# Attention scores Q·Kᵀ on one core: one store per head against two stores per three heads

## The chip, the cores and the metric

The kernel runs on one core of a Trainium2 chip. The metric is device time in microseconds (us) of one execution. The kernel before takes 1063.33 us, the median of three runs (1063.1 to 1064.34).

## The reference

```python
batch, n_heads, seq, head_dim = 8, 12, 1024, 64
q, k = 0.1 * randn(batch, n_heads, seq, head_dim)   # float32
out = np.einsum('bhid,bhjd->bhij', q, k)            # float32, 8 x 12 x 1024 x 1024
```

There are 96 heads. Each has Q and K of 1024 rows by 64 (256 KB each) and a result of 1024 x 1024 float32 (4 MB). Read are 50.3 MB, written 402.65 MB. Nothing is reduced on the chip: every product goes out.

## The kernel before, in words

A head's result leaves in one store. Output row 8p + t of a head lies in partition p at place t, so a store moves 128 pieces of 32 KB, one per partition, each contiguous in HBM (`scores`, line 185, issued by SyncE, called SP). The tile that it leaves from, `o_sb`, is one of three (`out_pool`, bufs=3).

To fill it, TensorE (PE) multiplies one weight tile of Q with the keys: contraction over the 64 values of `d`, 128 rows of Q, 512 keys at a time, four matmuls into a PSUM tile of 2048 columns (line 171). ScalarE (ACT) copies that to `o_sb` (line 181), four copies a head. PSUM holds two such tiles. Only the very first head uses four smaller PSUM tiles, copied by ACT and VectorE (DVE) in turn (line 179).

Q and K have to be turned, so that `d` lies along the partitions, and made float16. The 96 heads are cut into blocks of 2, 2, 4, 8, 8 and then six times 12 heads (`sizes`).

- The two blocks of 2 are loaded by head (`load_head`, line 84), cast by GpSimd (POOL, line 97) and transposed on PE, eight 128 x 128 transposes for each of Q and K (line 151), with a DVE or ACT copy out of PSUM (line 154). Both heads of a block sit side by side, 64 partitions each.
- The other blocks are loaded whole, Q and K in one DMA each (line 73). POOL casts them in quarters of 32 partitions into `half_sb` (line 127, five buffers), and DVE transposes blocks of 32 x 32 (line 145), writing them straight where PE wants them: the write goes along `i` in `dst = ... "c (i r) -> c r i"`, with R rows (32 to 96 elements of 2 bytes) from one element to the next.

What orders the work: every instruction is pinned in program order on its engine. The lists in `block` say after which matmul group of which head a transpose of the next block stands (`side`), and `LOADS` says after which head ACT issues the next two loads. SP carries the first loads of Q and all stores; ACT's queue carries the first loads of K and all later loads. A load waits for one of the two input buffers (`in_pool`), that is for POOL's casts. At the start the first 8 heads' inputs (4 MB) are loaded into the first `o_sb` buffer (`early`), and the 8 heads of block 3 (4 MB) into `x_sb`, all before the first store is issued.

Of the kernel before, what the change touches and what calls it, by code (L numbers as in the profile page):

```python
# [13 lines left out]
def kernel(  # L14
# [11 lines left out]
    GMAX = 4  # L26
    assert D == 64 and NT == 8 and BH % (2 * GMAX) == 0

# [4 lines left out]
    sizes = [2, 2, 4, 8, 8] + [12] * ((BH - 24) // 12)  # L33
    assert sum(sizes) == BH
    PE_BLOCKS = 2
    NMAX = max(sizes)
    CHUNK = 48 * 32

    consts = ctx.enter_context(tc.tile_pool(name="consts", bufs=1))
    ident = consts.tile([P, P], F16)  # L40

    in_pool = ctx.enter_context(tc.tile_pool(name="in_pool", bufs=2))
    half_pool = ctx.enter_context(tc.tile_pool(name="half_pool", bufs=5))
    tr_pool = ctx.enter_context(tc.tile_pool(name="tr_pool", bufs=2))
# [3 lines left out]

    def half_tile():
        half_sb = half_pool.tile([P, CHUNK], F16, tag="half")  # L50
        return half_sb

    class Block:

        def __init__(self, first, N, by_pe):
            self.first, self.N, self.by_pe = first, N, by_pe
            self.R = N * S // P
            self.elems = self.R * D  # L60
            self.raw = [None] * 2
            self.rows = [None] * 2
            self.halves = {}
            self.cut = max(1, self.R * 32 // CHUNK + (self.R * 32 % CHUNK > 0))

        def load(self, x, eng):
            if self.raw[x] is None:
                x_sb = in_pool.tile([P, self.elems], F32, tag="x")
                self.raw[x] = x_sb
            start = self.first * S  # L70
            src = (qf, kf)[x][start : start + self.N * S]
            pin(
                eng.dma_start(  # L73
                    out=self.raw[x], in_=src.rearrange("(p r) d -> p (r d)", p=P)
                )
            )

        def load_head(self, n, x, eng):

            start = (self.first + n) * S  # L80
            src = (qf, kf)[x][start : start + S]
            m = S * D // P
            pin(
                eng.dma_start(  # L84
                    out=self.raw[x][:, n * m : (n + 1) * m],
                    in_=src.rearrange("(p r) d -> p (r d)", p=P),
                )
            )

        def cast_rows(self, x):  # L90
            n = S * D // P
            self.rows[x] = half_tile()[:, : 2 * n].rearrange(
                "p (r h d) -> p r h d", h=2, d=D
            )
            for half in range(2):
                pin(
                    nc.gpsimd.tensor_copy(  # L97
                        out=self.rows[x][:, :, half],
                        in_=self.raw[x][:, half * n : (half + 1) * n].rearrange(
                            "p (r d) -> p r d", d=D  # L100
                        ),
                    )
                )

        def chunks(self):
            return [
                (x, part, c)
                for x in range(2)
                for part in range(2)
                for c in range(self.cut)  # L110
            ]

        def cast_quads(self, x, part, c):

            m = self.R // self.cut
            half_sb = half_tile()[:, : m * 32]
            self.halves[x, part, c] = half_sb  # L120
            raw = self.raw[x].rearrange("p (r h d) -> p r h d", h=2, d=32)
            for half in range(2):
                b = 2 * half + part
                for h in range(2):
                    q0 = 32 * (2 * half + h)
                    pin(
                        nc.gpsimd.tensor_copy(  # L127
                            out=half_sb[q0 : q0 + 32].rearrange(
                                "p (r d) -> p r d", d=32
                            ),  # L130
                            in_=raw[32 * b : 32 * b + 32, c * m : (c + 1) * m, h],
                        )
                    )

        def alloc(self):
            self.qT = tr_pool.tile([P, NMAX * S // 2], F16, tag="qT")
            self.kT = tr_pool.tile([P, NMAX * S // 2], F16, tag="kT")

        def transpose_quads(self, x, part, c):
            src = self.halves[x, part, c].rearrange("p (r i) -> p r i", i=32)  # L140
            n, m = self.N * S // 4, self.R // self.cut
            dst = (self.qT, self.kT)[x][:, part * n : (part + 1) * n].rearrange(
                "c (i r) -> c r i", i=32
            )[:, c * m : (c + 1) * m]
            pin(nc.vector.transpose(out=dst, in_=src))  # L145

        def transpose_rows(self, x, ps_pool, copy):
            ps = ps_pool.tile([P, S], F32, tag="po")
            t_ps = ps.bitcast(F16)[:, : NT * P].rearrange("c (t m) -> c t m", m=P)
            for t in range(NT):  # L150
                pin(nc.tensor.transpose(t_ps[:, t], self.rows[x][:, t], ident))  # L151
            dst = (self.qT, self.kT)[x][:, :S].rearrange("c (m t) -> c m t", t=NT)
            src = t_ps.rearrange("c t m -> c m t")
            pin(copy(out=dst, in_=src))  # L154

        def scores(self, n, side, ps_pool, w):

            half, g = divmod(n, self.N // 2)
            cs = slice(half * D, (half + 1) * D)

            qT = self.qT.rearrange("c (g m t) -> c g t m", t=NT, m=P)
            kT = self.kT.rearrange("c (g j) -> c g j", j=S)
            o_sb = out_pool.tile([P, NT, S], F32, tag="out")
            for u in range(NT // w):
                ps = ps_pool.tile([P, w * S], F32, tag="po")
                for tt in range(w):
                    for j in range(2):
                        js = slice(j * 512, (j + 1) * 512)
                        at = tt * S + j * 512
                        pin(  # L170
                            nc.tensor.matmul(  # L171
                                ps[:, at : at + 512],
                                qT[cs, g, w * u + tt],
                                kT[cs, g, js],
                            )
                        )
                dst = o_sb[:, w * u : w * u + w].rearrange("p t j -> p (t j)")
                if w == 1 and u % 2:
                    pin(nc.vector.tensor_copy(out=dst, in_=ps))  # L179
                else:  # L180
                    pin(nc.scalar.copy(out=dst, in_=ps))  # L181
                for do in side.get(u, []):
                    do()
            pin(
                nc.sync.dma_start(
                    out=of[self.first + n].rearrange("(p t) j -> p (t j)", p=P),
                    in_=o_sb.rearrange("p t j -> p (t j)"),
                )
            )

    blocks, first = [], 0
    for i, N in enumerate(sizes):
        blocks.append(Block(first, N, i < PE_BLOCKS))
        first += N

    early = out_pool.tile([P, NT, S], F32, tag="out")
    raw = early.rearrange("p t j -> p (t j)")
    at = 0
    for b in blocks[:3]:
        for x in range(2):  # L200
            b.raw[x] = raw[:, at : at + b.elems]
            at += b.elems
        if b.by_pe:
            for n in range(b.N):
                for x in range(2):
                    b.load_head(n, x, (nc.sync, nc.scalar)[x])
        else:
            for x in range(2):
                b.load(x, (nc.sync, nc.scalar)[x])
    stream = [(b, x) for b in blocks[3:] for x in range(2)]  # L210

    def next_load(eng):
        if stream:
            b, x = stream.pop(0)
            b.load(x, eng)

    for x in range(2):
        next_load((nc.sync, nc.scalar)[x])
    make_identity(nc, ident)

    casts = [
        (i, c) for i in range(PE_BLOCKS, len(blocks)) for c in blocks[i].chunks()
    ]

    def to_half(last):
        while casts:
            i, c = casts[0]
            if i > last or (blocks[i], c[0]) in stream:
                return
            blocks[i].cast_quads(*c)  # L230
            casts.pop(0)

    for b in blocks[:PE_BLOCKS]:
        for x in range(2):
            b.cast_rows(x)
# [39 lines left out]
    for i in range(1, len(blocks)):  # L275
        if i + 1 < len(blocks):
            blocks[i + 1].alloc()
# [31 lines left out]
```

## Time and profile before

| | |
|---|---|
| median of three runs | 1063.33 us |
| span of the profiled execution | 1061.8 us |
| DMA engines moved | 453.25 MB, mean 427 GB/s over the span |
| PE busy | 701.3 us (66%) |
| ACT busy | 697.6 us (66%) |
| DVE busy | 471.5 us (44%) |
| POOL busy | 368.3 us (35%) |
| stores | 96 of 4096 KB, 21.8 us from issue to landing |

The profiled execution's own time is its span, first instruction to last, 1061.8 us; the median of the runs without profile lies 1.5 us above it. Busy shares are means over the whole span. The DMA figures count the packets of the core's 16 DMA engines; the queue q1 is SP's, q10 is ACT's.

### The profile page before, as it was taken

The page shows a single profiled execution, that of the slowest core. Times are in us where ns is not written, and L with a number is a line of the kernel's source. Part 1 is how long each engine was busy: PE and PEld are TensorE (multiplying, and loading weights), DVE is VectorE, ACT ScalarE, POOL GpSimd, SP SyncE. Part 2 cuts the span into 40 slices and gives each one's busy share as a digit, 9 for nine tenths or more (in the row PEclk, how much of TensorE's full clock was granted, in tenths as well). Part 3 has the DMA queues.
Part 4 walks back from the last instruction along what each step waited for, and adds up shares of the span by engine and source line. Part 5 has one row for each costly group of instructions (what it writes and reads, how often), then busy time and mean ns, then how long its engine had stood idle before and what let it go on. Part 6 is the DMA issues. An engine that isn't in the chain of part 4 may idle for free.

```text
span 1061.8 us, 4282 instructions
## 1 busy us (share of the span) xinstructions
PE 701.3 (66%) x1568; PEld 241.6 (23%) x1568; DVE 471.5 (44%) x75; ACT 697.6 (66%) x386; POOL 368.3 (35%) x286
## 2 busy tenths in 40 slices
PE   6866755755677367773677836777367777778770
PEld 2322211211222122221222212222122222222220
DVE  2999601991696007960079600795007950000000
ACT  4856745755777366774677746777467777777771
POOL 6959128607630463303733046330463200000000
DMA  9999999999999999999999999999999999999997
GB/s 385 428 429 435 433 431 435 435 422 440 428 430 432 432 430 432 435 422 429 431 433 431 415 436 431 433 435 422 428 434 435 434 432 432 434 433 427 434 431 311
DMA packets 17588, 453.25 MB, mean 427 GB/s; under 512 B 1952, under 2 KB 1952, under 8 KB 2976
## 3 DMA queue, kind: packets, MB, share of 16 engines
q1 hardware_dynamic: 14688, 406.85, 89.1%
q10 hardware_dynamic: 2880, 46.14, 10.4%
q8 instruction: 12, 0.20, 0.1%
q14 instruction: 8, 0.07, 0.0%
HBM read 50.33 MB, written 402.65 MB: 427 GB/s over the span
## 4 chain that ended last, share of the span: by engine, by line
DMA 70%; ACT 17%; PE 7%; DVE 2%; issue 1%; POOL 1%; ACTq 0%; SPq 0%
DMA out_dram<-o_sb 70%; ACT o_sb L181 17%; PE ps L171 7%; DVE qT L145 1%; DVE kT L145 1%; DMA early<-in_q_dram 0%; POOL half_sb L127 0%; PE ps L151 0%; POOL half_sb L97 0%; DVE kT L154 0%; DVE o_sb L179 0%; ACTq L181 0%; ACT kT L154 0%; SPq L84 0%; ACTq L73 0%
## 5 line engine op out<-in xcount | busy, mean ns | idle before, releaser
L181 ACT COPY o_sb<-ps 128x2048 f32<-128x2048 f32 (+1 forms) x384 | 695.3, 1860 | 334.7 <-DMA out_dram<-o_sb 298.4
L171 PE MATMUL ps<-kT,qT 64*128 64x512 f16 x1536 | 697.2, 617 | 329.4 <-ACT o_sb L181 325.6
L127 POOL CAST half_sb<-x_sb 32x1536 f16<-32x1536 f32 (+1 forms) x256 | 346.5, 1353 | 455.1 <-DMA x_sb<-in_q_dram 318.3
L171 PEld LDWEIGHTS <-qT 64*128 64x128 f16 x1536 | 238.4, 157 | 786.3 <-issue 781.9
L145 DVE STREAM_TRANSPOSE qT<-half_sb 128x1536 f16<-128x1536 f16 (+1 forms) x34 | 232.8, 7140 | 372.2 <-issue 372.2
L145 DVE STREAM_TRANSPOSE kT<-half_sb 128x1536 f16<-128x1536 f16 (+1 forms) x34 | 234.2, 7181 | 0.0
L127 POOL CAST half_sb<-early 32x1024 f16<-32x1024 f32 x16 | 16.5, 1033 | 4.0 <-DMA early<-in_q_dram 3.3
L151 PE MATMUL ps<-ident,half_sb 128*128 128x128 f16 x32 | 4.1, 309 | 6.7 <-POOL half_sb L97 6.1
L154 DVE COPY qT<-ps 128x1024 f16<-128x1024 f16 x2 | 2.4, 1224 | 12.3 <-PE ps L151 12.3
L179 DVE COPY o_sb<-ps 128x1024 f32<-128x1024 f32 x4 | 4.9, 1224 | 4.3 <-PE ps L171 4.3
L97 POOL CAST half_sb<-early 128x512 f16<-128x512 f32 x8 | 4.6, 613 | 4.1 <-DMA early<-in_q_dram 4.1
L151 PEld LDWEIGHTS <-half_sb 128*128 128x128 f16 x32 | 3.2, 139 | 8.6 <-POOL half_sb L97 6.5
L154 ACT ACT_TABLE_LOAD x1 | 1.3, 1283 | 5.8 <-DMA early<-in_q_dram 5.8
L154 DVE COPY kT<-ps 128x1024 f16<-128x1024 f16 x1 | 1.2, 1224 | 4.3 <-PE ps L151 4.3
L154 ACT COPY kT<-ps 128x1024 f16<-128x1024 f16 x1 | 1.0, 1012 | 1.2 <-PE ps L151 1.2
masks.py:199 POOL TENSOR_SCALAR_AFFINE_SELECT ident<-ident 128x128 f16<-128x128 f16 x1 | 0.3, 292 | 0.1
masks.py:197 POOL MEMSET ident<- 128x128 f16 x1 | 0.2, 204 | 0.3 <-POOLq L293 0.3
L293 POOL MEMSET const-float32-0.0<- 128x1 f32 x1 | 0.1, 98 | 0.2 <-issue 0.2
L293 POOL MEMSET const-uint8-127<- 128x1 uint8 x1 | 0.1, 101 | 0.0
L293 POOL MEMSET const-bfloat16-1.0<- 128x1 bf16 x1 | 0.1, 100 | 0.0
L293 POOL MEMSET const-float32-1.0<- 128x1 f32 x1 | 0.1, 98 | 0.0
## 6 DMA issues: line engine op xcount, KB each, us to landing
out_dram<-o_sb SPq DMA_DIRECT2D x96, 4096.0 KB, 21.8
x_sb<-in_q_dram ACTq DMA_DIRECT2D x6, 3072.0 KB, 22.8
x_sb<-in_k_dram ACTq DMA_DIRECT2D x6, 3072.0 KB, 39.6
x_sb<-in_k_dram ACTq DMA_DIRECT2D x2, 2048.0 KB, 22.2
x_sb<-in_q_dram SPq DMA_DIRECT2D x1, 2048.0 KB, 18.0
x_sb<-in_q_dram ACTq DMA_DIRECT2D x1, 2048.0 KB, 19.0
early<-in_k_dram ACTq DMA_DIRECT2D x4, 256.0 KB, 5.0
early<-in_q_dram SPq DMA_DIRECT2D x4, 256.0 KB, 4.7
```

Of the source, the lines that this page charges most:

```text
L97: nc.gpsimd.tensor_copy(out=self.rows[x][:, :, half], in_=self.raw[x][:, half * n : (half + 1) * n].rearrange("p (r d) -> p r d", d=D),)
L127: nc.gpsimd.tensor_copy(out=half_sb[q0 : q0 + 32].rearrange("p (r d) -> p r d", d=32), in_=raw[32 * b : 32 * b + 32, c * m : (c + 1) * m, h],)
L145: pin(nc.vector.transpose(out=dst, in_=src))
L151: pin(nc.tensor.transpose(t_ps[:, t], self.rows[x][:, t], ident))
L154: pin(copy(out=dst, in_=src))
L171: nc.tensor.matmul(ps[:, at : at + 512], qT[cs, g, w * u + tt], kT[cs, g, js],)
L179: pin(nc.vector.tensor_copy(out=dst, in_=ps))
L181: pin(nc.scalar.copy(out=dst, in_=ps))
L293: nc = _bacc.Bacc("TRN2", target_bir_lowering=False, num_devices=1)
```

## The change

Heads 0 to 5 are handled as three pairs, in the way of the old 2-head blocks (loaded by head, transposed on PE, one 4 MB store a head). Heads 6 to 95 become 15 units of six heads. In a unit, three heads go out in two stores: output rows are numbered through the three heads (3072), 1536 go into one `o_sb` with 12 rows per partition, so a store moves 128 pieces of 48 KB (6 MB). A store thus holds one head and a half, and the partition where one head ends and the next begins lies inside a weight tile.

That is met so: the keys of two heads are stacked, one head in the upper 64 partitions, the other in the lower 64 (`keys`, `kk_sb`), and the matmul contracts over all 128 partitions. The Q tiles `z_upper` and `z_lower` have each column (a row of Q) in the half that belongs to its head and zeros in the other half, so that each output row meets its own keys alone. The zeros are written once (`memset`, lines 257 and 292).

DVE's transpose no longer writes where PE reads. It writes a dense tile `t_sb` (`turn`, line 177), and copies bring each piece to its place in `zs` or `kk_sb` (`place`, line 209), the keys of the middle head twice. `place` has 20 copies for each group of three heads, 7168 columns together (3072 of Q, 4096 of K), reading 2-byte values 64 bytes apart (`"c (r i) -> c i r"`) and writing densely.

Loads of a unit are 1.5 MB each for Q and K (12 KB per partition). There are now 66 stores, 12 loads of 256 KB and 30 of 1.5 MB; before there were 96 stores, 8 loads of 256 KB, 2 of 1 MB, 4 of 2 MB and 12 of 3 MB. Before the first store, the loads of 12 heads are issued (the six early ones and unit 0) instead of those of 16.

The core of the diff (removed lines of the old block class are left out; they stand in the listing above):

```diff
-    sizes = [2, 2, 4, 8, 8] + [12] * ((BH - 24) // 12)
+    FIRST = 6
+    UNIT = 6
+    T3 = 12
+    SPAN = P * T3
+    QUAD = 32
+    ROWS = UNIT * S // P
+    UNITS = (BH - FIRST) // UNIT
+    LOAD_AT = 3
...
+    z_upper = consts.tile([P, 3 * S], F16)
+    z_lower = consts.tile([P, 3 * S], F16)
+    zs = [z_upper, z_lower]
...
-    half_pool = ctx.enter_context(tc.tile_pool(name="half_pool", bufs=5))
-    tr_pool = ctx.enter_context(tc.tile_pool(name="tr_pool", bufs=2))
+    half_pool = ctx.enter_context(tc.tile_pool(name="half_pool", bufs=2))
+    tr_pool = ctx.enter_context(tc.tile_pool(name="tr_pool", bufs=4))
+    k_pool = ctx.enter_context(tc.tile_pool(name="k_pool", bufs=2))
...
+        def turn(self, x, part):
+            t_sb = turned_tile()
+            self.turned[x, part] = t_sb
+            src = self.halves[x, part].rearrange("p (r i) -> p r i", i=QUAD)
+            pin(nc.vector.transpose(out=t_sb.rearrange("c (r i) -> c r i", i=QUAD), in_=src))
+
+        def place(self, side, x, part):
...
+            own = slice(side * D, (side + 1) * D)
+            other = slice((1 - side) * D, (2 - side) * D)
+            src = self.turned[x, part][own].rearrange("c (r i) -> c i r", i=QUAD)
...
+                cs = other if head == 1 else own
+                if x == 0:
+                    places = [zs[side][cs, at : at + count]]
+                else:
+                    g = at - head * S
+                    sets = (0, 1) if head == 1 else (head // 2,)
+                    places = [
+                        self.keys[side][cs, m * S + g : m * S + g + count] for m in sets
+                    ]
+                for dst in places:
+                    pin(
+                        nc.vector.tensor_copy(
+                            out=dst.rearrange("c (i r) -> c i r", r=some.shape[2]), in_=some
+                        )
+                    )
+                row += count
+
+        def scores(self, side, g, todo, ps_pool):
+            weights = zs[side][:, g * SPAN : (g + 1) * SPAN].rearrange("c (m t) -> c t m", t=T3)
+            keys = self.keys[side][:, g * S : (g + 1) * S]
+            o_sb = out_tile()
+            for u in range(T3 // 2):
+                products(o_sb, 2 * u, 2, weights, keys, ps_pool, nc.scalar.copy)
+                for do in todo.get(u, []):
+                    do()
+            start = self.start + (2 * side + g) * SPAN
+            rows = out.rearrange("b h i j -> (b h i) j")[start : start + SPAN]
+            pin(
+                nc.sync.dma_start(
+                    out=rows.rearrange("(p t) j -> p (t j)", p=P),
+                    in_=o_sb.rearrange("p t j -> p (t j)"),
+                )
+            )
...
+    def turn_pair(n):
+        return {
+            2 * x: [lambda x=x: pairs[n].transpose(x, pool, nc.vector.tensor_copy)]
+            for x in range(2)
+        }
+
+    pairs[0].scores(1, turn_pair(1), pool, 2)
+    pairs[1].scores(0, turn_pair(2), pool, 2)
+    pairs[1].scores(
+        1, {1 + u: [lambda c=order[u]: units[0].turn(*c)] for u in range(2)}, pool, 2
+    )
+    for n in range(2):
+        todo = {
+            u: [lambda c=order[2 * n + u]: units[0].place(0, *c)] for u in range(2)
+        }
+        if n == 0:
+            for u in range(2):
+                todo[u].append(lambda c=order[2 + u]: units[0].turn(*c))
+        else:
+            todo[2] = [lambda x=x: units[1].load(x, nc.scalar) for x in range(2)]
+        pairs[2].scores(n, todo, pool, 2)
+    pin(nc.gpsimd.memset(z_lower, 0.0))
+
+    for k, unit in enumerate(units):
+        nxt = units[k + 1] if k + 1 < UNITS else None
+        if nxt:
+            for c in order:
+                nxt.cast(*c)
+        unit.scores(0, 0, {u: [lambda c=c: unit.place(1, *c)] for u, c in enumerate(order)}, pool)
+        todo = {}
+        if nxt:
+            todo = {u: [lambda c=c: nxt.turn(*c)] for u, c in enumerate(order)}
+        unit.scores(0, 1, todo, pool)
+        todo = {}
+        if nxt:
+            todo = {u: [lambda c=c: nxt.place(0, *c)] for u, c in enumerate(order)}
+        if k + 2 < UNITS:
+            for x in range(2):
+                todo[LOAD_AT] = todo[LOAD_AT] + [lambda x=x: units[k + 2].load(x, nc.scalar)]
+        unit.scores(1, 0, todo, pool)
+        unit.scores(1, 1, {}, pool)
```

In the changed program, on DVE each unit has 4 transposes and 40 copies; PE, ACT and POOL have nearly the same numbers of matmuls, copies and casts per head as before.

## The prediction

> **What bounds the kernel now.** I read the page first: the slices (part 2), the queues (part 3) and the chain that ended last (part 4).
>
> ```profile
> DMA  9999999999999999999999999999999999999997
> GB/s 385 428 429 435 433 431 435 435 422 440 428 430 432 432 430 432 435 422 429 431 433 431 415 436 431 433 435 422 428 434 435 434 432 432 434 433 427 434 431 311
> ...
> q1 hardware_dynamic: 14688, 406.85, 89.1%
> q10 hardware_dynamic: 2880, 46.14, 10.4%
> ...
> DMA 70%; ACT 17%; PE 7%; DVE 2%; issue 1%; POOL 1%; ACTq 0%; SPq 0%
> ```
>
> The two queues' packets fill 89.1 + 10.4 = 99.5% of all 16 engines' span. No slice but the last is below nine tenths. The chain calls ACT 17% and PE 7%, but that is the refill of a buffer while other stores move. So the DMA engines are the bound from start to end, and the next question is whether any of their time is lost. The stage view (busy time, granted clock, DMA share, GB/s) says where:
>
> ```profile
> 0.00:2.50 2.50, 0.00 (x0) 0.00 (x0) 0.00 (x0) 0.00 (x0) 0.70 (x6) 1.00 0.26 48
> 2.50:23.00 20.50, 13.69 (x48) 6.24 (x49) 6.42 (x6) 9.67 (x8) 13.92 (x17) 1.00 1.04 416
> 23.00:1039.40 1016.40, 687.63 (x1520) 235.41 (x1519) 465.11 (x70) 687.90 (x379) 353.72 (x263) 1.00 1.00 431
> 1039.40:1054.00 14.60, 0.00 (x0) 0.00 (x0) 0.00 (x0) 0.00 (x0) 0.00 (x0) 1.00 0.98 424
> 1054.00:1061.80 7.80, 0.00 (x0) 0.00 (x0) 0.00 (x0) 0.00 (x0) 0.00 (x0) 1.00 0.10 42
> ```
>
> Full from 2.5 us on, and empty only after 1054. A share of 0.10 in the last 7.8 us is one or two of 16 engines still at work: in the DMA records most engines end by 1052.5 to 1056.7, one at 1060.4. That engine sets the end. The pace of stores is read from SP's queue:
>
> ```profile
> 863.33 176.36 SPq L185 DMA_DIRECT2D out_dram<-o_sb  x19
> ```
>
> From the first to the last of 19 issues are 176.36 - 0.33 = 176.03 us, 9.78 us a store. In the DMA records a packet of 32 KB lasts 1213 ns, and the next starts 4 ns before it ends: eight for each engine are 9.67 us, and 15 engines keep that pace; the late one needs 9.78.
>
> **Part by part.** The sum is made against the span, 1061.8; the median is 1.5 us above, and the difference is added to it.
>
> *1. Fewer, larger pieces: -0.6 us.* The records give 309, 611, 912 and 1213 ns for 8, 16, 24 and 32 KB, a straight line with 7.7 ns left at size nought, of which 4 overlap. Packets of stores go from 96x8 = 768 to 6x8 + 60x8 = 528 an engine: -240 x 4 ns = -1.0. Those of loads go from 208 to 336: +0.5. A DMA's end packet takes 9 ns, and 122 become 108: -0.1. The bytes are the same. So nothing is to be had in the steady stage; it is full already. Were 48 KB cut up on the way, this term would be nought or a little above, no more.
>
> A rule of the Trainium skill speaks for more (DMA: Bandwidth & Descriptors, Anatomy of one DMA): a DMA costs about 2.0 us fixed plus its bytes at 436 GB/s. Paid one by one, that would be 11.6 us for a 4 MB store, and 14 fewer DMAs would give 28 us. The pace of 9.78 us disagrees: with stores queued, the fixed part is covered.
>
> *2. The start: +5.8 us.* Here the cover goes. Today loads fill the engines until about 22.8 us (where the first 32 KB packet starts), though the first store is issued at 17.69. The second and third stores are issued at 28.92 and 39.00; the DMA records end the first two at about 32.8 and 42.4. So each store comes in time, by some 2 to 3 us.
>
> ```profile
> 19.67 3.63 ACT L181 COPY o_sb<-ps 128x2048 f32<-128x2048 f32 x2 [3.13 <-PE ps L171]
> 25.26 3.63 ACT L181 COPY o_sb<-ps 128x2048 f32<-128x2048 f32 x2 [1.95 <-PE ps L171]
> 31.51 3.63 ACT L181 COPY o_sb<-ps 128x2048 f32<-128x2048 f32 x2 [2.62 <-PE ps L171]
> 35.33 3.65 ACT L181 COPY o_sb<-ps 128x2048 f32<-128x2048 f32 x2 [0.18 <-PE ps L171]
> ```
>
> In these rows of ACT a PE transpose between matmul groups costs the 1.95 and 2.62 us in brackets, against 0.18 without. The change does two things to this stage. First, loads ahead of the first store shrink by four heads, 2 MB. An engine's packets were 64x84 + 16x309 + 16x611 ns = 20.1 us; they become 96x84 + 16x457 ns (12 KB by the line above) = 15.4. Loads then end at about 18, not 22.8. Second, pair 2 is transposed on PE as well, and all four transposes stand inside heads 1 and 2 (after groups 0 and 2). Following the two PSUM tiles group by group (PE 1.85, ACT copy 1.85, transpose 1.0, DVE copy 1.22), head 1 goes out at 31.0 instead of 28.92, head 2 at 42.3 instead of 39.00. The first load is issued at 0.73 and its packet starts at 1.76; I take 1.1 us from issue to packet.
>
> Engines: store 0 from 18.9 to 28.6; store 1 from 32.1 (idle 3.5) to 41.8; store 2 from 43.4 (idle 1.6). Today store 2 follows at 42.4 with 4.8 us more of loads behind it: 43.4 - 42.4 + 4.8 = 5.8 us that are never made up, since the engines are full afterwards. Store 3 is issued at about 50, before 53.1, so the gaps stop.
>
> *3. DVE: nothing, if copies run as copies do now.* Rows by form:
>
> ```profile
> L145 DVE STREAM_TRANSPOSE qT<-half_sb 128x1536 f16<-128x1536 f16 x24 | 186.2, 8063 | 371.2 <-issue 371.2
> L145 DVE STREAM_TRANSPOSE qT<-half_sb 128x1024 f16<-128x1024 f16 x10 | 46.6, 4925 | 1.1 <-issue 1.1
> L154 DVE COPY qT<-ps 128x1024 f16<-128x1024 f16 x2 | 2.4, 1224 | 12.3 <-PE ps L151 12.3
> ```
>
> The added `place` copies read scattered and write densely, 14336 columns a unit. No row shows that from SBUF. Below: the PSUM copy, which also reads scattered (256 bytes apart), 1.2 ns a column, 17 us a unit. Above: the transpose, which writes scattered, 8063/1536 = 5.2 ns a column, 75 us. I take the copy, being the same operation, and 20 us with starts of small pieces. `turn` now writes densely: from 1.2 x 1536 = 1.8 us to today's 8.1; I take 1.8, since what was scattered in it is gone. That is 4x1.8 + 20 = 27 us a unit. A unit lasts 1050/16 = 65.6 us at the engines' pace, and covers it; it covers even 8.1 with 1.2 (32 + 20). ACT needs 6x1.9 = 11.4 us for a 48 KB buffer, the engines 14.5. POOL's casts of a unit are 16x1.46 = 23 us. ACT's load issues wait for those casts; behind them stand two copies of the running tile, and behind these a store, while two others are queued (29 us). The two memsets: 0.2 us for 128 columns of `ident` make at most 5 us for 3072, in POOL's idle time.
>
> *4. The end:* the last store is 6 MB, but the engines are full until it is gone; nothing.
>
> **Sum:** -0.6 + 5.8 = +5.2 us; span 1067.0, median 1063.3 + 5.2 = **1068.5 us**.
>
> **Rivals.** A measurement of this kernel can tell about 0.2% (2.1 us) from no change.
>
> *A. `turn` stays at 8.1 us.* Then unit 0 is late: DVE gets to it after pair 2's transposes (39.1). Four turns and four places (about 2.3 each) end at 39.1 + 32.4 + 9.3 = 80.8. The engines have work until 43.4 + 4x9.7 + 7.3 (unit 1's loads) = 89.5, and unit 0's first store needs 1.9 + 11.4 + 1.1 = 14.4 us after the last place: 95.2, idle 5.7. Median 1074; with places at twice the price 1081. It decides from a turn above 6.7 us. For it: same operation, same shape; against: only its write could make it four times a copy. Chance 0.12.
>
> *B. `place` at the price of scattered access.* At 5.2 ns a column DVE needs 75 + 7 = 82 us a unit against 65.6, and is the bound: 15 x 16.8 = 252 us more, about 1315. It decides above some 3.5 ns a column, because `place(0)` must also wait until the tile's last matmuls are done. For it: the transpose row is the only scattered SBUF access by DVE here; against: the PSUM copy. Chance 0.08.
>
> The Trainium skill (SBUF — State Buffer, Specifications) says so too: lines are 16 bytes, and an access that moves to a new line each time pays a penalty. It names no size. The scattered writes agree, the PSUM copy at 1.2 ns shows no such penalty, and for SBUF reads no run here shows it.
>
> *C. The late engine catches up: not slower.* It loses 0.1 us a store, and no other engine does; it is back at 9.68 in the last two stores, after ACT's last copy. I know no cause. If it hangs on 32 KB packets or on the number of stores, all engines end near the median one (1054.6 instead of 1060.4: -5.8) or near the first (-8). Median 1060.5 to 1062.7. It decides once the gain is more than 3.1 us, when we are within 0.2%. Against: it stops with compute, whose amount stays. Chance 0.13, of which 0.05 is faster by over 0.2%.
>
> *D. The start is hidden after all* (stores 1 and 2 come as early as today): 2.1 MB of loads move behind stores, nothing idles, 1062.7. Against: the transposes are in the program order. Chance 0.05.
>
> **How the numbers follow.** Forecast 0.62 (its own range 1065.5 to 1071: start +2.8 to +8). A 0.12, B 0.08, C 0.13, D 0.05. Slower: 0.62 + 0.12 + 0.08 = 0.82. Same: 0.08 of C and D = 0.13. Faster: 0.05. The range takes the forecast, A, and C's upper part: 1062.5 to 1081; out are B and the rest of C, some 0.15.
>
> **What would show it.** Right: DMA share below 0.9 in the stage 28 to 44 us, stores 1 and 2 issued near 31 and 42, then share 1.0 and 14.6 us a large store; L177 near 1.8 us, L209's 1008 columns near 1.2 us. Wrong: no gap in the start (D), a gap near 89 (A), DVE busy over 90% with ACT waiting on it (B), or engines that end together (C).

## The result, and the profile after

The changed kernel takes 1075.32 us, the median of four runs (1072.43 to 1076.62); on the same chip the kernel before took 1063.21 us. The ratio is 1.0108, 95% interval 1.0092 to 1.0125: slower by 12.1 us, where 5.2 were forecast. The profiled execution has a span of 1074.8 us, 12.9 more than before's 1061.8.

The page after, slices, queues and the chain (parts 2 to 4):

```profile
PEclk9996788686877868868778687887788887778875
DMA  9899999999999999999999999999999999999996
GB/s 371 351 412 439 432 435 424 424 424 430 446 411 430 430 427 427 428 430 430 428 427 430 440 418 423 439 427 428 433 427 438 408 439 428 436 439 421 434 432 276
...
q1 hardware_dynamic: 10512, 405.80, 88.2%
q10 hardware_dynamic: 5040, 47.19, 10.4%
...
DMA 70%; ACT 17%; PE 7%; POOL 1%; issue 1%; ACTq 1%; DVE 0%; SPq 0%; DVEq 0%; POOLq 0%
```

The DMA engines are the bound as before, but the second slice has fallen to 351 GB/s, and q1 has some 4200 packets fewer, q10 2160 more. The stages (start and end; time, busy time of PE, PEld, DVE, ACT, POOL, granted clock, DMA share, GB/s):

```profile
2.50:17.50 15.00, 9.05 (x32) 4.11 (x32) 6.02 (x5) 6.34 (x6) 9.51 (x13) 1.00 1.04 413
17.50:28.00 10.50, 7.96 (x30) 3.79 (x32) 2.54 (x3) 5.50 (x3) 9.23 (x7) 1.00 0.93 399
28.00:33.00 5.00, 2.94 (x16) 1.63 (x14) 0.64 (x2) 3.59 (x2) 2.45 (x2) 1.00 0.25 105
33.00:41.00 8.00, 6.90 (x24) 3.18 (x24) 3.60 (x4) 4.10 (x4) 0.00 (x0) 1.00 1.07 459
41.00:44.00 3.00, 1.61 (x5) 0.63 (x4) 3.00 (x2) 3.00 (x2) 2.90 (x2) 1.00 0.45 180
44.00:950.00 906.00, 448.25 (x1335) 199.34 (x1334) 506.19 (x617) 602.60 (x335) 354.43 (x232) 0.78 1.00 428
950.00:1040.00 90.00, 48.03 (x148) 21.66 (x146) 24.34 (x41) 66.74 (x38) 0.46 (x1) 0.81 1.01 436
```

Two losses can be read. Between 28 and 33 us, and between 41 and 44, the engines stand idle most of the time (share 0.25 and 0.45). And from 44 to 950 us, while units are loaded, they are busy all the time (share 1.00) and yet move 428 GB/s; once the loads are over, 436 at a share of 1.01, that is some 432 at 1.00. Before, the stage with loads ran at 431:

```profile
23.00:870.00 847.00, 562.92 (x1246) 192.80 (x1246) 465.11 (x70) 561.09 (x310) 353.72 (x263) 1.00 1.00 431
```

A busy engine that moves less has longer packets. The DMA records show which. Of the 7680 packets of 48 KB, the 4229 with no load packet in flight on any engine last 2 ns more than the usual 1815; the other 3451 last 38 ns more. It is not a little on every packet: of those beside a load, six in seven keep the usual time within 50 ns, and the rest are longer by 50 ns to 1 us.

So the loss can be kept in accounts. "Idle" is engine time without a packet from 2.1 to 60 us. "Lengthening" is the time of all packets above the usual for their size (84, 309, 460, 611, 912, 1213, 1815 ns for 2 to 48 KB), divided by 16. "Both" is the time after 30 us in which unit or block loads and stores have packets in flight together (the expectations of e2 and e4 go by an earlier count, 236 before and 414 after). "Mean end" is when the 16 engines end on average, "lag" how much later the last one ends.

| profiled execution, us | idle | lengthening | both | mean end | lag | last end |
|---|---|---|---|---|---|---|
| before | 0.1 | 5.8 | 210 | 1055.0 | 5.4 | 1060.4 |
| after | 6.0 | 11.2 | 401 | 1065.7 | 7.5 | 1073.2 |

They close: idle +5.9, lengthening +5.4 and the fewer packets -0.6 make +10.7, which is the mean end's 1065.7 - 1055.0; with +2.1 of lag, +12.8 at the last engine. All rests on one profiled execution of each kernel. A record does not name its engine, so packets were put in line by time, each behind the one that it follows; lengthening and both do not depend on that, the ends do.

Where the added time with both in flight comes from is seen at the loads' landing (part 6: form, KB each, us to landing), of before and of after:

```profile
x_sb<-in_q_dram ACTq DMA_DIRECT2D x6, 3072.0 KB, 22.8
x_sb<-in_k_dram ACTq DMA_DIRECT2D x6, 3072.0 KB, 39.6
```

```profile
x_sb<-in_k_dram ACTq DMA_DIRECT2D x15, 1536.0 KB, 42.0
x_sb<-in_q_dram ACTq DMA_DIRECT2D x14, 1536.0 KB, 23.5
```

Half the bytes take as long. An engine with packets in both queues mostly takes one of each in turn: in the records 1213, 912, 1213, 912 before, and a 12 KB packet between two of 48 KB after (some 2960 of 3580 load packets of the units stand right behind a store's). Q and K of 12 heads are 16 load packets an engine before, beside 16 stores' packets: 16 x (0.91 + 1.21) = 34 us. Now they are 32, each beside 1.82 us: 73 us. The records bear this estimate out: the loads of a block of 12 heads are under way for 33 to 37 us before, those of a unit of 6 for 35 to 38 after.

### The profile page after: what moved, and what is told of

Its sections match the earlier page's. It is cut to its first block, busy times and chain, and to the rows that moved or that the text cites. A ratio compares the mean times of both kernels' runs of the same rounds, so it can differ in the third digit from the quotient of the medians.

```text
span 1074.8 us, 4916 instructions
## 1 busy us (share of the span) xinstructions
PE 524.7 (49%) x1584; PEld 234.3 (22%) x1584; DVE 546.3 (51%) x669; ACT 693.4 (65%) x386; POOL 379.7 (35%) x260
## 4 chain that ended last, share of the span: by engine, by line
DMA 70%; ACT 17%; PE 7%; POOL 1%; issue 1%; ACTq 1%; DVE 0%; SPq 0%; DVEq 0%; POOLq 0%
DMA out_dram<-o_sb 67%; ACT o_sb L83 17%; PE ps L77 6%; DMA x_sb<-in_k_dram 3%; POOL half_sb L167 1%; DMA o_sb<-in_q_dram 0%; ACTq L156 0%; PE ps L123 0%; ACTq L337 0%; POOL half_sb L110 0%; DVE o_sb L83 0%; DVE kk_sb L125 0%; ACT kk_sb L125 0%; ACTq L83 0%; SPq L97 0%
## 5 line engine op out<-in xcount | busy, mean ns | idle before, releaser
L167 POOL CAST half_sb<-x_sb 32x1536 f16<-32x1536 f32 x240 | 366.8, 1528 | 555.8 <-DMA x_sb<-in_q_dram 419.9
L77 PE MATMUL ps<-kk_sb,z_upper 128*128 128x512 f16 x720 | 239.7, 472 | 274.6 <-ACT o_sb L83 274.1
L77 PE MATMUL ps<-kk_sb,z_lower 128*128 128x512 f16 x720 | 237.9, 469 | 223.2 <-ACT o_sb L83 222.8
L209 DVE COPY kk_sb<-t_sb 64x1008 f16<-64x1008 f16 (+1 forms) x360 | 268.6, 807 | 0.8
L177 DVE STREAM_TRANSPOSE t_sb<-half_sb 128x1536 f16<-128x1536 f16 x60 | 105.6, 1772 | 212.0 <-POOL half_sb L167 211.6
L77 PEld LDWEIGHTS <-z_upper 128*128 128x128 f16 x720 | 107.7, 150 | 407.0 <-issue 383.8
L77 PEld LDWEIGHTS <-z_lower 128*128 128x128 f16 (+1 forms) x752 | 112.3, 150 | 364.2 <-issue 340.4
L209 DVE COPY z_lower<-t_sb 64x1008 f16<-64x1008 f16 (+3 forms) x120 | 83.1, 735 | 201.2 <-PE ps L77 197.8
L209 DVE COPY z_upper<-t_sb 64x1008 f16<-64x1008 f16 (+3 forms) x120 | 81.6, 728 | 0.4
L77 PE MATMUL ps<-kk_sb 64*128 64x512 f16 x64 | 26.4, 622 | 7.6 <-ACT o_sb L83 3.9
```

The costliest lines, as they stand in the source:

```text
L77: nc.tensor.matmul(ps[:, tt * S + j : tt * S + j + 512], weights[:, t + tt], keys[:, j : j + 512],)
L167: nc.gpsimd.tensor_copy(out=half_sb[to : to + QUAD].rearrange("p (r d) -> p r d", d=32), in_=raw[b : b + QUAD, :, h],)
L177: pin(nc.vector.transpose(out=t_sb.rearrange("c (r i) -> c r i", i=QUAD), in_=src))
L209: nc.vector.tensor_copy(out=dst.rearrange("c (i r) -> c i r", r=some.shape[2]), in_=some)
```

## The experiments

Accounts of all profiled executions in one place; the columns are those above, the median and the ratio to before are from the timed runs.

| | median us | ratio, 95% | idle | lengthening | both | lag |
|---|---|---|---|---|---|---|
| after | 1075.32 | 1.0108 (1.0092 to 1.0125) | 6.0 | 11.2 | 401 | 7.5 |
| e1 start | 1073.08 | 1.0089 (1.0074 to 1.0104) | 3.2 | 14.3 | 412 | 1.2 |
| e2 before, blocks of 6 | 1067.15 | 1.0037 (1.0023 to 1.0052) | 0.2 | 9.6 | 325 | 4.6 |
| e3 loads on SP | 1072.55 | 1.0089 (1.0072 to 1.0105) | 6.2 | 6.7 | 146 | 8.0 |
| e4 stores cut in two | 1073.90 | 1.0102 (1.0087 to 1.0117) | 6.3 | 8.5 | 291 | 4.7 |
| e5 after, few loads | 998.81 | 0.9397 (0.9383 to 0.9411) | 6.6 | 6.1 | 102 | 8.1 |
| e6 before, few loads | 990.33 | 0.9312 (0.9296 to 0.9328) | 0.1 | 4.7 | 60 | 6.4 |
| e7 no place | 1076.81 | 1.0133 (1.0108 to 1.0157) | 6.7 | 12.4 | 399 | 4.2 |
| e8 start, loads on SP | 1069.02 | 1.0050 (1.0035 to 1.0065) | 3.3 | 5.9 | 166 | 8.1 |
| e9 before, loads on SP | 1066.12 | 1.0027 (1.0016 to 1.0039) | 0.1 | 5.7 | 73 | 8.1 |
| e10 start closed, SP | 1067.25 | 1.0038 (1.0025 to 1.0052) | 1.4 | 6.0 | 163 | 8.8 |

### e1: the start alone

```diff
-            2 * x: [lambda x=x: pairs[n].transpose(x, pool, nc.vector.tensor_copy)]
+            1 + 2 * x: [lambda x=x: pairs[n].transpose(x, pool, nc.vector.tensor_copy)]
...
-    pairs[1].scores(0, turn_pair(2), pool, 2)
...
+    pairs[1].scores(0, {}, pool, 2)
+    todo = turn_pair(2)
+    todo[3] = todo[3] + [lambda c=order[u]: units[0].turn(*c) for u in range(2)]
+    pairs[1].scores(1, todo, pool, 2)
```

> The changed kernel with the PE transposes of pairs 1 and 2 put back behind groups 1 and 3 (pair 2's into head 3 instead of head 2), nothing else moved. Start theory: store 1 is issued near 28.9 us and store 2 near 39, idle DMA time in the start falls from some 5.9 us to 2.5 to 3 us, and the run is about 3 us faster than the changed kernel (ratio to before near 1.008). Rival (the whole loss comes from the later stage, where loads run beside stores): the start gap closes, yet the time stays at the changed kernel's 1075 (ratio 1.011), as the engines would only wait elsewhere.

Idle time fell nearly as expected, 6.0 to 3.2 (2.5 to 3 forecast), and the median by 2.2 us, but the two ratios' intervals overlap. In the profiled run lengthening grew by 3.1, so the mean end came 0.4 us later, not earlier (1066.1), and lag fell by 6.3. Alone it decides little.

### e2: the kernel before with the small loads

```diff
-    sizes = [2, 2, 4, 8, 8] + [12] * ((BH - 24) // 12)
+    sizes = [2, 2, 4, 8, 8] + [6] * ((BH - 24) // 6)
...
-            if n == LOADS.get(i, 6):
+            if n == LOADS.get(i, 3):
```

> The kernel before with blocks of 6 heads instead of 12 from head 24 on (24 loads of 1.5 MB instead of 12 of 3 MB), stores still 32 KB per partition. Mixing theory (a store's packets get longer while the load queue has packets on the engines, so what counts is the time with both in flight): that time grows from 236 us to some 300 to 350 us, and the run is 1 to 2 us slower than before (ratio 1.001 to 1.002). Rival (12 KB loads are what costs, about 0.2 us each): 5 us slower (1.005). Rival (only 48 KB stores suffer): no difference (1.000).

4 us slower, with the stores untouched: half-size loads cost by themselves. The interval holds the first rival's 1.005 and leaves out the mixing theory's 1.001 to 1.002. The form of the loss is the theory's, though. It sits in the packets of the stores, 1223.6 ns on average instead of 1216.9, while the 12 KB packets last 460.7 ns, as usual: +3.8 us of lengthening for +115 us of both. The stage from 23 to 870 us, 431 GB/s before:

```profile
23.00:870.00 847.00, 566.03 (x1254) 192.39 (x1254) 400.39 (x64) 563.88 (x311) 330.59 (x248) 1.00 1.00 429
```

Time with both is not the whole of it: a 32 KB packet with a load in flight is 15 ns over the usual in before, beside 24 KB loads, and 34 ns here, beside 12 KB ones. By number of load packets, 3.8 us for 96 more an engine is 39 ns each, and after's 5.4 us for 128 more is 42, so a price for each load packet fits these two runs as well; e4 and e3 change the price with the loads' packets as they are.

### e3: loads in the stores' queue

```diff
-            todo[2] = [lambda x=x: units[1].load(x, nc.scalar) for x in range(2)]
+            todo[2] = [lambda x=x: units[1].load(x, nc.sync) for x in range(2)]
...
-                todo[LOAD_AT] = todo[LOAD_AT] + [lambda x=x: units[k + 2].load(x, nc.scalar)]
+                todo[LOAD_AT] = todo[LOAD_AT] + [lambda x=x: units[k + 2].load(x, nc.sync)]
```

> The changed kernel with all unit loads issued from SP's queue instead of ACT's, so that they stand in one line with the stores and no engine alternates between two queues. Mixing theory: 48 KB packets fall to a mean near 1817 ns from 1833, the eight late engines catch up, and the run is 5 to 8 us faster than the changed kernel (ratio 1.003 to 1.006). Rival (48 KB pieces, or DVE's copies, slow the engines): packets stay at 1833 ns and the time near 1075 (1.011).

The packets did what was expected: 48 KB packets fell from 1833 to 1817 ns, and the stage from 45 to 950 us, first after, then this run, rose from 428 to 431 GB/s:

```profile
45.00:950.00 905.00, 447.25 (x1333) 199.03 (x1332) 505.19 (x616) 601.78 (x334) 353.47 (x231) 0.78 1.00 428
```

```profile
45.00:950.00 905.00, 451.82 (x1342) 200.65 (x1341) 427.50 (x625) 605.77 (x335) 339.01 (x231) 0.77 1.00 431
```

The mean end came 4.4 us earlier (1061.3). Of the stores' gain a part went into the loads: 12 KB packets last 475.6 ns on average instead of 461.6, 3.4 us of lengthening an engine. The time came down by only 2.8 us, with intervals that overlap: one engine ended 8.0 us behind the mean and 4.2 behind the next. The expectation that the late engines catch up failed.

### e4: each large store as two DMAs

```diff
...
+            dst = rows.rearrange("(p t) j -> p (t j)", p=P)
+            flat = o_sb.rearrange("p t j -> p (t j)")
+            n = T3 * S // 2
+            for h in range(2):
+                cut = slice(h * n, (h + 1) * n)
+                pin(nc.sync.dma_start(out=dst[:, cut], in_=flat[:, cut]))
```

> The changed kernel with each 48 KB store issued as two DMAs of 24 KB per partition, one behind the other; all else is kept. Rival (the large packets are what costs): the time falls by 4 to 6 us (ratio 1.005 to 1.007). Mixing theory: loads now alternate with packets half as long, the time with both in flight falls from 414 us to about 300, and the time falls by 1 to 3 us (ratio 1.008 to 1.010). DVE theory (copies slow the engines): no change, 1.011.

Now 24 KB packets stand between the loads, and K lands after 27.1 us:

```profile
out_dram<-o_sb SPq DMA_DIRECT2D x120, 3072.0 KB, 36.9
...
x_sb<-in_k_dram ACTq DMA_DIRECT2D x15, 1536.0 KB, 27.1
```

Both fell to 291 us and lengthening to 8.5, as the mixing theory has it, with the loads unchanged. But the 7680 added packets (480 an engine, 4 ns each) and the 60 added end packets cost some 2.5 us of it back, idle time rose by 0.3, and the mean end is 0.4 us later than after's; the time fell by 1.4 us (intervals overlap) through a smaller lag, which no theory had forecast. So the packets bear the mixing theory out, and the time decides nothing.

### e5 and e6: both kernels with few loads

The loads of the last 60 heads are left out, and those heads are computed from inputs of an earlier unit or block.

```diff
 # after
+            if self.start >= (FIRST + 5 * UNIT) * S:
+                self.raw[x] = units[4].raw[x]
+                return
 # before
+            if self.first >= 36:
+                self.raw[x] = blocks[5].raw[x]
+                return
```

> The changed kernel without the loads of units 5 to 14 (60 heads, 31.5 MB): those units cast and multiply unit 4's inputs again, all else is kept. To be read beside the kernel before with the same 60 heads' loads left out. Mixing theory (store packets get longer only while loads are in flight beside them): time with both in flight falls from 401 to about 115 us, the lengthening of packets from 11 to about 5 us an engine; some 995 us, and 5 to 8 us above its partner, which is the start's 5.9 us and little else. Rival (48 KB pieces, DVE's copies or the matmuls over 128 rows slow the engines all the time): still 11 to 12 us above its partner.

> The kernel before without the loads of the last five blocks (60 heads, 31.5 MB), which cast and multiply the inputs of block 5 again. Mixing theory: 1063.1 less 10 loads x 8 packets x 0.912 us = 73 us and 2 to 3 us of longer packets, near 988 us. Rival: only the 73 us go, 990 us.

998.81 against 990.33: 8.5 us apart instead of 12. This is half a us outside the mixing theory's 5 to 8, and well off the rival's 11 to 12. By accounts, of e5 less e6, idle is 6.5, lengthening 1.4, packets -1.0 and lag 1.7.

Each against its full kernel says more. The same 60 heads' loads take 73 us of an engine's time by themselves. The changed kernel gains 76.5 us without them, and its lengthening falls by 5.1; the kernel before gains 73.0, just what e6's rival said, and its lengthening falls by 1.1. Both times are above the mixing theory's 995 and 988. So the loads cost the changed kernel more than their own time, and the kernel before hardly. Yet the stores are not all at their usual time here: in e6 a 32 KB packet with no load in flight is 4.2 ns over it, against 1.7 in before, and in e5 a 48 KB packet 5.6 ns, against 2.2 in after. No run shows why.

Where no loads run, 48 KB stores are as good as 32 KB ones: from 350 to 960 us, first e5, then e6,

```profile
350.00:960.00 610.00, 334.59 (x996) 148.98 (x996) 333.85 (x429) 451.60 (x250) 205.01 (x137) 0.79 1.00 433
```

```profile
350.00:960.00 610.00, 451.54 (x996) 154.71 (x994) 247.24 (x32) 451.83 (x249) 157.99 (x108) 1.00 1.00 431
```

433 and 431 GB/s, with DVE's copies and the 128-row matmuls running in the first.

### e7: without DVE's copies

From unit 1 on, the copies of `place` are left out, and every unit multiplies unit 0's Q tiles and keys.

```diff
+                if self.start > FIRST * S:
+                    self.keys[side] = units[0].keys[side]
...
+            if self.start > FIRST * S:
+                return
```

> The changed kernel without the copies of place for units 1 to 14: their matmuls use unit 0's Q tiles and keys again (560 DVE copies left out, some 410 us of DVE time). Mixing theory: no difference, 1073 to 1076 us (ratio 1.009 to 1.012). DVE theory (its copies slow DMA's access to SBUF): 5 us faster or more (1.006 or less).

DVE's busy time fell from 546 to 146 us:

```profile
PE 530.6 (49%) x1584; PEld 234.4 (22%) x1584; DVE 145.9 (14%) x109; ACT 694.0 (65%) x386; POOL 364.6 (34%) x260
```

The time did not (1076.81, 0.8 us over the expected range; one run took 1081.45). DVE's copies do not slow the DMA engines. The Trainium skill says as much (SBUF — State Buffer, SBUF: two separate sides): compute engines and DMA reach SBUF by different ports and cannot contend. Here the trace agrees: 12.4 us of lengthening without the copies, 11.2 with them.

### e8 and e10: the start, with loads on SP's queue

e8 puts the edits of e1 and e3 together. e10 adds to it that head 1, too, is copied out by ACT and DVE in turn:

```diff
         pairs[0].scores(0, {}, pool, 1)
+        turns = {
+            4 + 2 * x: [lambda x=x: pairs[1].transpose(x, pool, nc.vector.tensor_copy)]
+            for x in range(2)
+        }
+        pairs[0].scores(1, turns, pool, 1)
...
-    pairs[0].scores(1, turn_pair(1), pool, 2)
```

> Both helpful edits together: transposes of the pairs as in the first experiment, unit loads from SP's queue as in the third. Accounts by engine time: idle time in the start 3.2 us instead of 6.0, lengthening of packets 6.4 us instead of 11; if the two add up, some 1069 to 1070 us (ratio 1.006). Rival (one late engine sets the end whatever the mean is): 1072 us or more (1.009).

> The version with both edits, and head 1 also copied out by ACT and DVE in turn out of four small PSUM tiles, as head 0 is, with pair 1's transposes behind its groups 4 and 6. Start theory: store 1 is issued near 26 us, ahead of the end of store 0 (28.5), store 2 near 36; idle time in the start falls from 3.3 to about 1 us; 1066 to 1067.5 us (ratio 1.003 to 1.004). Rival (the start was paid for by waits later): no change, 1069.

Both came as expected in time; idle time in e10 is 1.4 where about 1 was forecast. SP's first three stores, e8, then e10 (start, time from the first to the end of the last issue):

```profile
18.15 21.64 SPq L139 DMA_DIRECT2D out_dram<-o_sb  x3
```

```profile
17.91 18.55 SPq L139 DMA_DIRECT2D out_dram<-o_sb  x3
```

Store 2 is issued at 39.5 and at 36.1 us, against 42.5 in the changed kernel. From e3 to e8 idle time falls by 2.9 us and the median by 3.5; from e8 to e10 by 1.9 and by 1.8. The mean ends move by 3.6 and 1.8 us. In these two steps what the engines idle in the start is lost at the end about one for one, and what is closed there comes back (e8's and e10's intervals overlap, e3's and e8's do not).

### e9: the kernel before with loads on SP's queue

```diff
-                side[1] = side.get(1, []) + [lambda: next_load(nc.scalar)] * 2
+                side[1] = side.get(1, []) + [lambda: next_load(nc.sync)] * 2
```

> The kernel before with its later loads issued from SP's queue instead of ACT's, nothing else moved. Mixing theory: time with loads and stores in flight falls from 210 to some 120 us; at 0.02 to 0.03 us lost per us that is 2 to 3 us less lengthening; the last engine may lag as before, so 1060 to 1063 us (ratio 0.998 to 1.000). Rival (SP's stores wait behind a load that waits for casts): 1065 us or more.

Slower by 3 us, a miss. Both fell to 73 us, but lengthening stayed at 5.7: it left the stores (1216.9 to 1214.5 ns) and went into the 24 KB load packets (929 to 942). The mean end is the same (1054.9). The 3 us are lag, 8.1 instead of 5.4. The time lies where the rival put it, but not for the rival's reason: stores that wait would leave the engines idle and move the mean end. In one line it is the loads that are slow, here those beside other engines' stores: a 24 KB packet is 1.6 ns over the usual with no store in flight, 38 ns beside one to seven and 123 beside eight or more. (e3's 12 KB packets do not order so: 18 ns with no store in flight.) No version tried with all its loads beats the kernel before.

## Why the prediction was wrong, point by point

**The bound** was read rightly: nothing but the engines' packets and gaps counts.

**Step 1 failed.** "The bytes are the same. So nothing is to be had in the steady stage; it is full already." The sum had -0.6 for it; it cost +5.4 of lengthening beside that -0.6. That is 5.4 of the 7.6 us by which the last engine's 12.8 exceeds the sum's 5.2; 2.1 are lag, which step 4 ("the engines are full until it is gone; nothing") had at nought. A full stage can still get slower, and the step counted packets at their median. The means were there to be seen: 32 KB packets at 1216.9 and 24 KB ones at 929.0, that is 4.6 of before's 5.8 us of lengthening. The step also changed the loads from 208 to 336 packets and asked only for their fixed cost, not how long they would run beside stores. e2 shows the loads' half size at work (+3.8 us of lengthening with 32 KB stores), e4 the stores' size (8.5 us with 24 KB packets, 11.2 with 48 KB). Measured from before, the runs with 12 KB loads in a queue of their own (after, e1, e2, e4 and e7) lose 0.03 to 0.04 us for each further us of both. The few loads of e5 and e6 do not fit that rate: e6 has 150 us less of both than before, and only 1.1 us less lengthening. So it is small loads in their own queue beside the stores that cost; why a read in flight makes a write's packet longer stays open. With one queue (e3 and e9) the stores keep their usual time, and the load packets are the longer ones.

The rule of the Trainium skill that the prediction weighed here (DMA: Bandwidth & Descriptors, Anatomy of one DMA) changes nothing in this: the section gives 2.0 us for DMAs issued from GpSimd, and these are issued from SP and ACT.

**Step 2 was right.** Store 1 was issued at 31.30 (31.0 forecast), store 2 at 42.47 (42.3), idle time 6.0 us (5.8). SP's queue:

```profile
17.68 13.96 SPq L139 DMA_DIRECT2D out_dram<-o_sb  x2
```

17.68 + 13.96 - 0.33 is 31.31, and the rows of ACT show the gaps of the transposes, once each between two copies:

```profile
23.82 3.64 ACT L83 COPY o_sb<-ps 128x2048 f32<-128x2048 f32 x2 [2.29 <-PE ps L77]
29.41 3.63 ACT L83 COPY o_sb<-ps 128x2048 f32<-128x2048 f32 x2 [1.95 <-PE ps L77]
34.99 3.63 ACT L83 COPY o_sb<-ps 128x2048 f32<-128x2048 f32 x2 [1.95 <-PE ps L77]
```

e8 and e10 confirm that it is lost at the end.

**Step 3 was right in its result.** `turn` takes 1.77 us, as taken. `place` was taken at 20 us a unit, and is (268.6 + 83.1 + 81.6)/15 = 28.9. By form:

```profile
L209 DVE COPY kk_sb<-t_sb 64x1008 f16<-64x1008 f16 x60 | 111.5, 1858 | 0.0
L177 DVE STREAM_TRANSPOSE t_sb<-half_sb 128x1536 f16<-128x1536 f16 x60 | 105.6, 1772 | 212.0 <-POOL half_sb L167 211.6
L209 DVE COPY kk_sb<-t_sb 64x32 f16<-64x32 f16 x120 | 38.3, 360 | 0.4
```

1.84 ns a column where 1.2 was expected, and 0.36 us for a piece of 32; over all pieces 2.0 ns a column. A unit's 65 us cover it.

**Rivals.** A and B are out by these rows; B's threshold of 3.5 ns was not reached. The rule of the Trainium skill that the prediction weighed (SBUF — State Buffer, Specifications) may have a part in that: scattered reads from SBUF cost 1.84 ns a column, against 1.2 from PSUM, but no run reads the same tile densely, so the size of a penalty is not shown. C is out for the changed kernel: its last engine lags 7.5 us, not less. But lag was no constant, and the prediction treated it as one. It runs from 1.2 to 8.8 us over the twelve profiled executions. That, and lengthening between 11.2 and 14.3 with the same loads, may be why the changed kernel's runs spread over 4 us and before's over 1.3; each kernel was profiled once, so this is not shown. D is out. The measured time lies outside the forecast's own range, 1065.5 to 1071, and inside the wide one only by the room left for A.

**Open:** the late engine. In e9 the stores land 9.68 us apart until 339 us, 9.78 from there to 1044 us wherever no load stands between, and 9.67 for the last two, after ACT's last copy (1041.9). Before, too, has 9.78 until its last two stores. All four runs with loads in SP's queue end with a lag of 8.0 to 8.8. No experiment found what makes it.

## What to carry to other kernels

A DMA-bound stage that is 100% busy need not be at its floor: compare the mean of the packets with the median, by size, and see beside what the longer ones run. Here two queues shared an engine packet by packet, so small load pieces beside large store pieces stretched the loads, and the stores paid. When pieces are resized, work out how long the loads are under way, (load piece + store piece) x number of load pieces: for a unit that is 36 us after and 22 in e4, for 6 heads in e2 27, and the records, after the first unit, have 35 to 38, 22 to 23 and 26 to 28. And in such a kernel the first stores are a schedule of their own: loads that ran ahead of them were filling the engines, and a gap there was not made up.

## What the hardware showed that was not expected

The granted clock has to be read with care. First the matmuls of after, then of before (count, then min/median/max ns):

```profile
L77 PE MATMUL ps<-kk_sb,z_upper x720: 376/379/634, 63.4 to 1009.1; 128*128 128x512 f16 x180
```

```profile
L171 PE MATMUL ps<-kT,qT x1536: 579/627/643, 9.4 to 1036.8; 64*128 64x512 f16 x192
```

The pages put a mean granted clock of 0.78 beside the first (44 to 950 us) and 1.00 beside the second, as if PE were faster at a lower clock. But the trace of before holds no record of the clock at all, and 1.00 is what a view prints where there is none; nor do those of e2, e6 and e9, the other kernels with 64 rows throughout. In after the clock goes back and forth between 1.00 and 0.50, and the matmuls with it, first from 112.6 to 126.3 us at 1.00, then from 126.4 to 132.9 at 0.50:

```profile
L77 PE MATMUL ps<-kk_sb,z_upper x8: 377/378/379, 120.0 to 122.5; 128*128 128x512 f16 x8
```

```profile
L77 PE MATMUL ps<-kk_sb,z_upper x8: 586/634/634, 129.3 to 132.3; 128*128 128x512 f16 x8
```

The 627 ns of before are near the 634 at 0.50 and far from 378. This suggests that PE ran at the lower clock all through the kernel before, and that contraction over 128 rows raised it about half of the time; without a clock record it is not shown. It saves nothing here, as ACT and the DMA engines behind it set the pace.

And a DVE transpose of 128 x 1536 takes 1.77 us when it writes densely, and 8.06 when its 2-byte writes lie 192 bytes apart (7.57 in e2, where they lie 96 apart).
